# First loads on two queues, another deal of the fill, and attention outputs stored one step later, in a fused two-branch attention layer

## The chip, the cores and the metric

The kernel runs on one core of a Trainium2 chip. A core has a matmul engine (TensorE, PE in the profile; PEld is its weight load), a vector engine (VectorE, DVE), an activation engine (ScalarE, ACT), a general engine (GpSimd, POOL) and SyncE (SP), which here only issues transfers between device memory and on-chip memory (SBUF). Matmuls write to a second on-chip memory, PSUM. The metric is the device time of the whole program in microseconds (us).

## The reference

One layer: normalise the rows of x, project them with one matrix w_in into the q, k, v and gate columns of two attention branches, attend, multiply by the gate, project each branch, merge and project out. There are 1024 prompt tokens and 64 sample tokens, the latter with 512 cached keys. All numbers are float32.

```python
h = rms_norm(x, norm_w) @ w_in
sb_q, sb_k, sb_v, sb_z, cb_q, cb_k, cb_v, cb_z, g_sb, g_cb = split(h)
# branch sb, stick-breaking: z = q.k / 8, keys s < t
w = exp(log_sigmoid(z) + (reverse_cumsum(log_keep) - log_keep))     # log_keep = log_sigmoid(-z) where s < t
o_sb = w @ v
# branch cb: keys of the last 8 chunks of 64 and the own one, softmax with a clipped relative bias
o_cb = softmax(q.k / 8 + rel_bias) @ v                              # q and k with an RMS norm per head
b_sb = (o_sb * silu(z_sb)) @ w_proj_sb
b_cb = (o_cb * silu(z_cb)) @ w_proj_cb
y = x + (sigmoid(g_sb) * b_sb + sigmoid(g_cb) * b_cb) @ w_out
```

## The kernel before

Every float32 matmul operand is split into a high and a low part, and three products of the parts are summed; that is why q, k and the projections exist as pairs of tiles (hi and lo).

The program has three parts. First come the norm and nearly all columns of w_in; the results go to device memory (`d_qT`, `d_kT`, `d_z`, `d_g` and so on). The last four column blocks of w_in, called units, are left over as filler. Then comes the attention, and after it the second branch's projection and the output projection. The change touches the attention part.

**Steps.** The attention runs over a list `seq` of 136 steps, written out by hand: branch sb and then branch cb; in each, four pairs of heads p; in each pair the sample tile (t = 8, both heads in one step) and then the eight prompt tiles t = 0 to 7, once for each head. A pair is 17 steps. Step i issues, in this order: for cb, `soft` of step i-1 and `mid` of step i-2; `qk(i)` (the scores, L1039, into PSUM tiles z, then for sb two sigmoids on ACT and for cb the bias add on DVE); loads for later steps (`load_z` and `prefetch`); for sb, `mid` of step i-1 (the scan on DVE, with its constants in a PSUM tile `imp`, and the product on POOL); `flush`, which issues postponed stores; a piece of fill; the product with v that has come due (`av`, L1134); the transposes of step i-4 (`tr`, L1100, LAG = 4); and another piece of fill. A prompt step of sb has 128(t+1) keys, one of cb at most 640, the sample step 576.

**Fill.** `fill(n)` puts n matmuls of the filler between the attention's own. The filler is the four units (72 matmuls each in three groups of 24, L782) and then `proj_sb`, the first branch's projection (288 matmuls in groups of 12, L881). Seventy-two are issued before step 0. How many follow in each step is the table `plan`. Before the change `plan` comes, for both branches, from a model (`share`) of what a step costs on PE and on the other engines; it deals 168 matmuls to the sb steps and 228 to the cb steps. The last unit's second group may not start before `late["sb"]` is set, since it loads the first branch's outputs (`load_og`, tiles `ot`, L838). Each output is then split by `og_hi` on ACT (L842) and `og_lo` on DVE or POOL (L847), called between filler matmuls (`og_step`). The filler's `ot`, gate (`gt`, L861) and weight (`wraw`, L109) loads are issued as its generator reaches them.

**Queues.** All loads and stores of this part are issued by SP, in program order; an issue that has to wait holds all issues behind it. Of the load helpers, `place_k` and `place_q` issue four transfers each through `rdma` (L51): `ks` (prompt keys, 256 KB each), `kss` (cached and new sample keys, 128 KB and 16 KB each), `sq` (queries of three prompt tiles, 192 KB each) and `sqs` (sample queries, 32 KB each). `load_v` issues three (L735 to L737), `load_z` one gate tile `zt` (L1117). `av` multiplies its result into `zt` (L1139) and postpones the store of that tile (L695). Every transfer takes one of eight completion counters in turn, and it is not issued before the counter's last transfer has landed.

**Start of the attention.** The loads for step 0 and 1 are issued between pieces of 12 filler matmuls, so the filler's own stores and weight load stand between them in SP's order.

## Time and profile before

| | us |
|---|---|
| median of 3 runs | 1021.68 (1019.37 to 1023.84) |
| the profiled execution | 1022.05 |
| its span, first to last instruction | 1020.1 |
| PE idle in the whole span (1020.10 less 970.01 busy) | 50.1 |
| first filler matmul; first score matmul; second score step | 523.26; 535.10; 546.64 |
| second branch's first score step; last score matmul | 692.58; 851.6 |

Outside the span lie 1022.05 - 1020.1 = 1.95 us. A row of the view of waits reads: engine, operation and line that waited, what ended the wait; us in total, times, longest. A row of the view of stretches reads: stretch, its length, busy us (and instructions) of PE, PEld, DVE, ACT and POOL, the clock granted to PE (1.00 is full), busy share of the transfer engines, GB/s. A row of the view in order of time reads: start, length, engine, line, operation, tiles, shapes, count, and in brackets the idle time before it and what ended it. SPq is SP's issue of a transfer; its length is the issue, not the transfer.

### The profile page before, as it was taken

The numbers are of one execution on the slowest core, as the hardware profiler recorded it, in microseconds if no ns is written. First come the engines' busy times: TensorE is split into PE (matmuls) and PEld (weight loads), VectorE is DVE, ScalarE is ACT, GpSimd is POOL, SyncE is SP. The second block draws the span as 40 slices with busy tenths as digits, with TensorE's granted clock in tenths as the row PEclk, the third lists the DMA queues.
The fourth block names the chain that finished last, engine by engine and source line by source line (L and its number), as shares of the span: only waits on it lengthen the run. The fifth ranks groups of instructions, "written<-read, shape, count | busy, mean of one in ns | idle before, by whom it ended". The sixth has DMA issues, their size and how long they took to land.

```text
span 1020.1 us, 20722 instructions
## 1 busy us (share of the span) xinstructions
PE 970.0 (95%) x7616; PEld 919.0 (90%) x7616; DVE 620.3 (61%) x1259; ACT 496.8 (49%) x1110; POOL 426.7 (42%) x432
## 2 busy tenths in 40 slices
PE   5999999999999999999995998999899799999998
PEld 5999999999999999999995777777787787999998
DVE  5466663985545556233214888887677665589735
ACT  6544442444344333333324775776776665456320
POOL 3376663115544445444423655653110100377452
PEclk9999999999999999999997999999999999999999
DMA  6736468335654333334229756767878662663642
GB/s 230 222 124 208 165 239 289 122 103 168 189 164 152 105 114 113 96 97 128 86 82 241 211 155 162 185 168 198 236 201 218 176 180 82 216 209 99 192 130 91
DMA packets 172197, 166.99 MB, mean 164 GB/s; under 512 B 34688, under 2 KB 157952, under 8 KB 171968
## 3 DMA queue, kind: packets, MB, share of 16 engines
q1 hardware_dynamic: 163376, 157.34, 51.8%
q10 hardware_dynamic: 8720, 8.33, 2.5%
q8 instruction: 60, 0.98, 0.4%
q14 instruction: 41, 0.34, 0.1%
HBM read 106.89 MB, written 58.72 MB: 162 GB/s over the span
## 4 chain that ended last, share of the span: by engine, by line
PE 84%; DMA 4%; ACT 4%; SPq 3%; DVE 2%; issue 1%; POOL 0%; ACTq 0%; POOLq 0%; DVEq 0%
PE b L642 29%; PE acc L472 19%; PE b L1485 7%; PE o L1134 7%; PE pt L1100 5%; PE b L923 5%; PE z L1039 4%; PE acc L881 4%; PE acc L782 2%; SPq L51 2%; DMA wraw<-in_w_proj_sb_dram 1%; ACT wT L1109 1%; DVE wT L1111 1%; ACT be L1043 1%; PE pk L357 1%
## 5 line engine op out<-in xcount | busy, mean ns | idle before, releaser
L1069 POOL TENSOR_TENSOR be<-be,kp 128x128 f32<-128x128 f32 (+8 forms) x68 | 82.0, 1206 | 77.3 <-DVE kp L1067 41.3
L1039 PE MATMUL z<-ks,sq 128*128 128x320 f32 (+5 forms) x384 | 88.8, 340 | 13.4 <-DMA d_gcb<-sg 10.3
L1100 PE MATMUL pt<-ident,be 128*128 128x128 f32 (+1 forms) x568 | 89.3, 280 | 8.8 <-DVE wT L1111 4.4
L1100 PEld LDWEIGHTS pt<-ident,be 128*128 128x128 f32 (+1 forms) x568 | 65.1, 141 | 23.1 <-issue 9.7
L122 POOL TENSOR_TENSOR wlo<-wraw,whi 128x1024 fp32r<-128x1024 f32 x18 | 43.6, 2422 | 95.5 <-ACT whi L115 95.3
L1067 DVE TENSOR_TENSOR_SCAN kp<-kp,acc 128x512 f32<-128x512 f32 (+6 forms) x60 | 76.8, 1280 | 2.1
L1039 PEld LDWEIGHTS z<-ks,sq 128*128 128x128 f32 x384 | 63.9, 192 | 15.6 <-DMA sq<-d_qsbT 10.5
L472 PE MATMUL acc<-whi,xa 128*128 128x256 f32 x256 | 74.2, 292 | 0.0
L1134 PE MATMUL o<-wT,vp 128*64 128x256 f32 (+1 forms) x608 | 71.5, 365 | 1.5 <-DVE wT L1111 1.2
L650 DVE TENSOR_TENSOR u<-b,s 128x256 f32<-128x256 f32 (+1 forms) x56 | 24.4, 440 | 78.7 <-PE b L642 77.0
L472 PE MATMUL acc<-wlox,xm 128*128 128x256 f32 x256 | 70.7, 278 | 0.0
L472 PE MATMUL acc<-whi,xm 128*128 128x256 f32 x256 | 70.7, 278 | 0.0
L1111 DVE COPY wT<-pt 128x512 f32<-128x512 f32 (+3 forms) x125 | 63.2, 517 | 12.2 <-PE pt L1100 11.4
L472 PE MATMUL acc<-wlo,xa 128*128 128x256 f32 x256 | 70.7, 278 | 0.0
L472 PE MATMUL acc<-whix,xb 128*128 128x256 f32 x256 | 70.6, 278 | 0.0
L472 PE MATMUL acc<-whix,xm 128*128 128x256 f32 x256 | 70.6, 278 | 0.0
L1134 PEld LDWEIGHTS o<-wT,vp 128*64 128x64 f32 x608 | 45.9, 140 | 25.5 <-issue 6.1
L1042 ACT ACTIVATE kp<-z 128x384 f32<-128x384 f32 (+6 forms) x104 | 52.8, 508 | 23.7 <-PE z L1039 21.2
L1109 ACT ACTIVATE wT<-pt 128x512 f32<-128x512 f32 (+3 forms) x75 | 36.7, 489 | 49.0 <-PE pt L1100 48.8
L442 POOL TENSOR_TENSOR whix<-ws,whix 128x512 fp32r<-128x512 f32 x28 | 37.0, 1320 | 41.9 <-ACT whix L441 41.9
L1043 ACT ACTIVATE be<-z 128x384 f32<-128x384 f32 (+6 forms) x104 | 53.3, 512 | 0.0
L1072 ACT ACTIVATE be<-be,sm 128x640 f32<-128x640 f32 (+5 forms) x68 | 47.1, 693 | 11.4 <-DVE sm L1071 11.3
(299 smaller groups left out, 3225.0 us busy)
## 6 DMA issues: line engine op xcount, KB each, us to landing
wraw<-in_w_in_dram SPq DMA_DIRECT2D x31, 512.0 KB, 4.3
wrawx<-in_w_in_dram SPq DMA_DIRECT2D x17, 512.0 KB, 4.5
sq<-d_qsbT SPq DMA_DIRECT2D x32, 192.0 KB, 3.8
sq<-d_qcbT SPq DMA_DIRECT2D x32, 192.0 KB, 4.8
xt<-in_x_prompt_dram SPq DMA_DIRECT2D x8, 512.0 KB, 5.4
d_kcbT<-hl SPq DMA_DIRECT2D x8, 512.0 KB, 4.6
d_qcbT<-hl SPq DMA_DIRECT2D x8, 512.0 KB, 5.5
d_ksbT<-hl SPq DMA_DIRECT2D x16, 256.0 KB, 2.5
```

What stands on the lines that cost most here:

```text
L472: TE.matmul(ps, x, w, start=m == 0, stop=m == len(steps) - 1)
L642: TE.matmul(ps[:, :m], w[:, hl_, k], right[s](x)[:, k, a:b], start=s < 3 and k == 0 and e == 0, stop=k == 3 and e == 2, skip_group_check=s ...
L923: TE.matmul(pp[uu][:, :n], w[:, p, uu * 128:uu * 128 + 128], g[:, a:e], start=p == 0 and m == 0, stop=p == NPAIR - 1 and m == 2)
L1039: TE.matmul(z[:, :m], s[:, e, q0:q0 + 128], ks[:, h, o + x:o + y], start=e == parts[0][0], stop=e == parts[-1][0])
L1042: A.activation(kp[:r, x:y], z[:r, :m], AF.Sigmoid, scale=-0.125)
L1043: A.activation(be[:r, x:y], z[:r, :m], AF.Sigmoid, scale=0.125)
L1067: V.tensor_tensor_scan(kp[:, m - 1::-1], kp[:, m - 1::-1], imp[:, 192:193].to_broadcast([128, m]), kp[:, m:m + 1], op0=OP.mult, op1=OP.add)
L1069: G.tensor_tensor(out=be[:r, :n], in0=be[:r, :n], in1=kp[:r, 1:n + 1], op=OP.mult)
L1100: TE.transpose(pt[:kr, x, :r], be[:r, kb * 128:kb * 128 + kr], ident[:r, :r])
L1111: V.tensor_copy(w[:, sl:sl + m, q0:q0 + r], pt[:, :m, :r])
L1134: TE.matmul(o[hd * 64:hd * 64 + 64, c0:c1], vv[:kr, kb, hd * 64:hd * 64 + 64], wT[b, p, j, hd, s // 4][:kr, s % 4, c0:c1] if j < 4 else wT ...
L1485: TE.matmul(ps[:, t], left[s](xs_, k)[:, ts_], wt_[:, k], start=s < 3 and t == k == e == 0, stop=k == 3 and e == 2, skip_group_check=s > 2 ...
```

## The change

Four things are changed.

1. The first loads: `rdma`, `place_k`, `place_q`, `load_q` and `load_k` can issue from another engine. All loads for steps 0 and 1 now come before the 72 filler matmuls. `sqs` and `ks` are issued by ACT, the others by SP.
2. The fill: the cb steps get 12 matmuls at once and then 240 more in proportion to the number of keys plus 150 (`need`). The sb steps still go by the model, with 144 instead of 168.
3. The store of an attention output waits for one more `flush` (`store_later(..., 1)`), the tiles `zt` have four buffers instead of three, and `late["sb"]` is set one step later to match.
4. Nothing is added to or taken from the work: 576 filler matmuls in all, 72 ahead and 108 after the steps, as before, up to one by rounding.

The table `plan`, in filler matmuls per pair of 17 steps:

| pair | before | after |
|---|---|---|
| sb 0 / 1 / 2 / 3 | 57 / 37 / 37 / 37 | 51 / 31 / 31 / 31 |
| cb 0 / 1 / 2 / 3 | 55 / 57 / 57 / 59 | 71 / 60 / 60 / 60 |
| cb 1, its 17 steps | 0 0 0 2 0 0 2 8 7 3 8 6 7 0 3 6 5 | 5 1 2 2 2 3 3 4 3 5 4 5 4 4 5 4 4 |

SP at the start of the attention, before. `kss`, `sqs`, `ks` and `sq` are keys and queries of steps 0 and 1, `vp` and `vs` the values, `d_gcb<-sg` the filler's stores, `wraw` the filler's weights; "x4" is four transfers.

```order
L51 DMA kss<-d_csbT_77 64x512 x4
L51 DMA kss<-d_ksbT_69 64x64 x4
L51 DMA sqs<-d_qsbT_61 64x2x64 x4
L695 DMA d_gcb_105<-sg 128x384
L51 DMA ks<-d_ksbT_69 64x1024 x4
L109 DMA wraw<-in_w_in_dram 128x8x128
L51 DMA sq_7093<-d_qsbT_61 64x2x384 x4
L695 DMA d_gcb_105<-sg 128x128
L695 DMA d_gcb_105<-sg 128x32
L695 DMA d_gcb_105<-sg 128x224
L735 DMA vp<-d_sbv 128x8x128
```

SP at the same place, after:

```order
L51 DMA kss<-d_csbT_77 64x512 x4
L51 DMA kss<-d_ksbT_69 64x64 x4
L51 DMA sq_7041<-d_qsbT_61 64x2x384 x4
L735 DMA vp<-d_sbv 128x8x128
L736 DMA vs<-in_cache_sb_v_dram 128x4x128
L737 DMA vs<-d_sbv 64x128
L1117 DMA zt<-d_zsb_85 128x64
L695 DMA d_gcb_105<-sg 128x384
L109 DMA wraw<-in_w_in_dram 128x8x128
L695 DMA d_gcb_105<-sg 128x128
L695 DMA d_gcb_105<-sg 128x32
L695 DMA d_gcb_105<-sg 128x224
```

The other half stands on ACT, after the last evacuation of the part before (`hl`) and ahead of the filler's first evacuation (`sg`). In brackets is what each issue waits for: DMAHW0 to DMAHW7 are the eight completion counters.

```order
L580 ACTIVATE hl<-u_6830 128x288 [waits DMAHW0_49,DMAHW7_49,DVE_49,Activation_49]
L51 DMA sqs<-d_qsbT_61 64x2x64 [waits Pool_49]
L51 DMA sqs<-d_qsbT_61 64x2x64
L51 DMA sqs<-d_qsbT_61 64x2x64 [waits DMAHW1_49]
L51 DMA sqs<-d_qsbT_61 64x2x64 [waits DMAHW3_49]
L51 DMA ks<-d_ksbT_69 64x1024 [waits DMAHW5_49]
L51 DMA ks<-d_ksbT_69 64x1024 [waits DMAHW0_49]
L51 DMA ks<-d_ksbT_69 64x1024 [waits DMAHW3_49]
L51 DMA ks<-d_ksbT_69 64x1024 [waits DMAHW7_49]
L757 ACTIVATE sg<-acc 128x384 [waits PE_49]
```

So `sqs` and `ks` no longer queue behind `kss`, `sq` stands ahead of the filler's traffic, and the values ahead of the filler's weights.

SP between the third and the fourth pair of branch cb, before; `bias` and `bsm` are the bias rows of the next pair, `sqs` the queries that its first step needs:

```order
L51 DMA kss<-d_ccbT_84 64x512 x4
L51 DMA kss<-d_kcbT_84 64x64 x4
L861 DMA gt<-d_gsb_95 128x384
L861 DMA gt<-d_gsb_96 128x384
L109 DMA wraw<-in_w_proj_sb_dram 128x4x256
L1170 DMA bias<-d_rb_123 128x640
L1170 DMA bias<-d_rb_124 128x640
L1178 DMA bsm<-d_rb_123 64x576
L1178 DMA bsm<-d_rb_124 64x576
L695 DMA d_ocb_115<-zt 128x256
L1117 DMA zt<-d_zcb_91 128x256
L51 DMA sqs<-d_qcbT_68 64x2x64 x4
```

and after:

```order
L109 DMA wraw<-in_w_proj_sb_dram 128x4x256
L695 DMA d_ocb_114<-zt 128x256
L1117 DMA zt<-d_zcb_91 128x256
L51 DMA kss<-d_ccbT_84 64x512 x4
L51 DMA kss<-d_kcbT_84 64x64 x4
L695 DMA d_ocb_115<-zt 128x64
L1170 DMA bias<-d_rb_123 128x640
L1170 DMA bias<-d_rb_124 128x640
L1178 DMA bsm<-d_rb_123 64x576
L1178 DMA bsm<-d_rb_124 64x576
L1117 DMA zt<-d_zcb_91 128x256
L51 DMA sqs<-d_qcbT_68 64x2x64 x4
```

The filler's gate and weight loads left the place between `kss` and `sqs`, and the stores `d_ocb` moved behind the loads of the next step.

PE at the first steps of the second pair of cb, before (`z` scores, `o` the product with v, `pt` transposes, `acc` filler):

```order
L1039 MATMUL z<-kss,sqs 128x288 x8
L1134 MATMUL o<-wT,vp 64x256 x8
L1134 MATMUL o<-wT,vp 64x128 x4
L1100 MATMUL pt<-ident,be 128x128 x5
L1039 MATMUL z<-ks,sq_9702 128x128 x2
L1100 MATMUL pt<-ident,be 128x128 x5
L1039 MATMUL z<-ks,sq_9702 128x128 x2
L1100 MATMUL pt<-ident,be 128x128 x5
L1039 MATMUL z<-ks,sq_9702 128x256 x2
L881 MATMUL acc<-xb,whi 128x384
L1100 MATMUL pt<-ident,be 128x128 x5
```

and after:

```order
L1039 MATMUL z<-kss,sqs 128x288 x8
L782 MATMUL acc<-xm,wlo 128x320
L881 MATMUL acc<-xa,whi 128x384
L1134 MATMUL o<-wT,vp 64x256 x8
L1134 MATMUL o<-wT,vp 64x128 x4
L1100 MATMUL pt<-ident,be 128x128 x5
L881 MATMUL acc<-xb,whi 128x384
L881 MATMUL acc<-xa,wlo 128x384
L881 MATMUL acc<-xa,whi 128x384
L1039 MATMUL z<-ks,sq_9685 128x128 x2
L1100 MATMUL pt<-ident,be 128x128 x5
L881 MATMUL acc<-xb,whi 128x384
```

Each short step now has filler of its own.

The diff, with the parts that only pass the engine on left out:

```diff
-    def rdma(out, in_):
+    def rdma(out, in_, eng=SP):
         out, in_ = (a if isinstance(a, bass.AP) else a[:] for a in (out, in_))
-        SP.dma_start(out.bitcast(F32), in_.bitcast(F32))
+        eng.dma_start(out.bitcast(F32), in_.bitcast(F32))
...
-    def store_later(dst, src):
-        deferred.append((0, lambda: SP.dma_start(dst, src)))
+    def store_later(dst, src, n=0):
+        deferred.append((n, lambda: SP.dma_start(dst, src)))
...
-        zt = am.tile([128, 256], F32, name="zt", bufs=3)
+        zt = am.tile([128, 256], F32, name="zt", bufs=4)
...
-        store_later(d_o[b][p][:, 256 * j:256 * j + nq], os[:, :nq])
+        store_later(d_o[b][p][:, 256 * j:256 * j + nq], os[:, :nq], 1)
...
     load_k("sb", 0, 1)
-    for f in (lambda: load_q("sb", 0, 3), lambda: load_k("sb", 0, 0), lambda: load_q("sb", 0, 0),
-              lambda: (load_v("sb", 0), load_z("sb", 0, 4)), lambda: None, lambda: None):
+    load_q("sb", 0, 3, A)
+    load_q("sb", 0, 0)
+    load_k("sb", 0, 0, A)
+    load_v("sb", 0)
+    load_z("sb", 0, 4)
+    for _ in range(6):
         fill(12)
         flush()
-        f()
...
     plan = {}
-    for b, budget in (("sb", 72 * (len(units) - 1) - 48), ("cb", 48 + FP)):
+    steps = [i for i in range(len(seq)) if seq[i][0] == "cb"]
+    need = [band(*seq[i][::2])[1] + 150 for i in steps]
+    acc = 12.0
+    for i, n in zip(steps, need):
+        acc += (60 + FP) * n / sum(need)
+        plan[i] = int(acc)
+        acc -= plan[i]
+    for b, budget in (("sb", 72 * (len(units) - 1) - 72),):
...
-        if i == len(seq) // 2 + LAG + 1:
+        if i == len(seq) // 2 + LAG + 2:
             late["sb"] = True
```

More of the change, by code (lines that the diff above doesn't have):

```diff
@@ L692, in flush, with place_k, place_q @@
                 deferred.append((n - 1, f))
-    def store_later(dst, src):
-        deferred.append((0, lambda: SP.dma_start(dst, src)))
-    def place_k(dst, src, o0, o1, a, b):
+    def store_later(dst, src, n=0):
+        deferred.append((n, lambda: SP.dma_start(dst, src)))
+    def place_k(dst, src, o0, o1, a, b, eng=SP):
         for hd in range(2):
             for m in range(2):
-                rdma(dst[m * 64:m * 64 + 64, hd, a:b], src[hd * 64:hd * 64 + 64, m, o0:o1])
-    def place_q(dst, src, o0, o1):
+                rdma(dst[m * 64:m * 64 + 64, hd, a:b], src[hd * 64:hd * 64 + 64, m, o0:o1], eng)
+    def place_q(dst, src, o0, o1, eng=SP):
         for hd in range(2):
@@ L708, in place_q @@
                 rdma(dst[dup * 64:dup * 64 + 64, 2 * hd:2 * hd + 2, c:c + o1 - o0],
-                     src[hd * 64:hd * 64 + 64, :, o0:o1])
+                     src[hd * 64:hd * 64 + 64, :, o0:o1], eng)
     SQ, KS, VP, BI, st, wT, zts = {}, {}, {}, {}, {}, {}, {}
@@ L738, in load_v, with load_q @@
         VP[b, p] = (vp, vs)
-    def load_q(b, p, ci):
+    def load_q(b, p, ci, eng=SP):
         x, y = CH[ci] if ci < 3 else (NP, T)
@@ L743, in load_q, with load_k @@
             y = min(y, NP)
-        place_q(alloc_q((b, p), ci), d_qT[b][p][:], x, y)
-    def load_k(b, p, s):
+        place_q(alloc_q((b, p), ci), d_qT[b][p][:], x, y, eng)
+    def load_k(b, p, s, eng=SP):
         if s:
@@ L750, in load_k @@
         else:
-            place_k(alloc_k((b, p), 0), d_kT[b][p][:], 0, NP, 0, NP)
+            place_k(alloc_k((b, p), 0), d_kT[b][p][:], 0, NP, 0, NP, eng)
     def ev_act(func, dst, ci, a, b, ps):
```

## The prediction

> **What bounds the kernel now.** I read the page's chain first, then what PE waited for, then the stretches around the long waits, then SP's issues there.

> ```profile
> PE 84%; DMA 4%; ACT 4%; SPq 3%; DVE 2%; issue 1%; POOL 0%; ACTq 0%; POOLq 0%; DVEq 0%
> ```
> ```profile
> PE z L1039 <- DMA d_gcb<-sg: 10.3, 1, 10.3
> ...
> PE z L1039 <- DMA sqs<-d_qcbT: 4.9, 1, 4.9
> PE pt L1100 <- DVE wT L1111: 4.4, 9, 0.8
> ...
> PE z L1039 <- DVE sm L1045: 1.8, 1, 1.8
> ...
> PE z L1039 <- DMA sq<-d_qcbT: 1.3, 2, 1.1
> ```

> PE carries 84% of the chain, so the change can only win by filling PE's holes; it removes no matmul. The rows shown lie in the attention, at places that the change touches. How large the holes are, with the slow clock behind them, the stretches show:

> ```profile
> 535.10:546.64 11.54, 1.21 (x10) 1.00 (x9) 2.37 (x6) 1.75 (x5) 1.24 (x2) 0.71 1.02 225
> 546.64:550.20 3.56, 3.56 (x13) 3.56 (x14) 0.84 (x2) 0.89 (x4) 0.45 (x2) 0.51 0.99 278
> ...
> 722.80:727.20 4.40, 1.67 (x8) 0.69 (x6) 2.31 (x9) 4.17 (x9) 0.29 (x2) 1.00 1.02 302
> 727.20:732.00 4.80, 4.78 (x24) 3.24 (x24) 2.22 (x8) 3.18 (x7) 2.29 (x4) 0.64 0.55 157
> ...
> 810.30:815.20 4.90, 0.00 (x0) 0.01 (x1) 0.84 (x3) 1.32 (x3) 1.92 (x5) 0.77 0.48 122
> 815.20:818.50 3.30, 3.28 (x14) 2.64 (x16) 0.99 (x4) 0.00 (x0) 1.01 (x1) 0.50 0.89 247
> 818.50:822.00 3.50, 3.31 (x29) 2.20 (x25) 0.75 (x4) 0.43 (x1) 0.00 (x0) 0.82 0.95 255
> ```

> **Term 1, the first loads.** SP's issues in order of time:

> ```profile
> 525.36 2.43 SPq L51 DMA_DIRECT2D kss<-d_csbT  x4
> 527.83 2.52 SPq L51 DMA_DIRECT2D kss<-d_ksbT  x4
> 530.45 3.15 SPq L51 DMA_DIRECT2D sqs<-d_qsbT  x4
> 533.70 0.53 SPq L695 DMA_DIRECT2D d_gcb<-sg  x1
> 534.28 2.38 SPq L51 DMA_DIRECT2D ks<-d_ksbT  x4
> 536.71 0.59 SPq L109 DMA_DIRECT2D wraw<-in_w_in_dram  x1
> 537.34 2.75 SPq L51 DMA_DIRECT2D sq<-d_qsbT  x4
> 540.19 2.60 SPq L695 DMA_DIRECT2D d_gcb<-sg  x3
> 545.22 0.37 SPq L735 DMA_DIRECT2D vp<-d_sbv  x1
> ```
> ```profile
> 525.00:530.00 5.00, 5.00 (x30) 5.00 (x30) 0.00 (x0) 1.44 (x2) 0.80 (x1) 1.00 0.44 140
> 530.00:535.00 5.00, 5.00 (x35) 5.00 (x34) 0.00 (x0) 0.49 (x1) 1.66 (x3) 1.00 0.22 56
> 535.00:540.00 5.00, 1.31 (x10) 1.08 (x8) 2.37 (x6) 1.75 (x5) 1.14 (x2) 0.99 0.94 230
> ...
> 555.00:560.00 5.00, 4.88 (x34) 3.89 (x32) 4.50 (x9) 4.58 (x12) 3.39 (x7) 1.00 1.05 241
> ```

> An issue takes about 0.6 us (2.43/4). The large transfers (`ks`, 1 MB; `sq`, 0.77 MB) stand behind `kss`, `sqs` and filler traffic, so the transfer engines idle until 534 (0.44 and 0.22 busy) and are then full, still so in 555 to 560. PE pays in 535 to 547. The values `vp` were issued at 545.22, which is when `wraw`, eight places ahead, had landed.

> ```profile
> 527.68 0.49 ACT L757 ACTIVATE sg<-acc 128x384 f32<-128x384 f32 x1 [3.23 <-PE acc L782]
> ```

> After, ACT is free at 524.45 (this first evacuation of the filler stood behind 3.23 us of idle time). It issues four `sqs` (to about 527) and four `ks`, of which the last waits for the fourth `kss`; ACT is done by about 531. The evacuation then comes some 3 us late; the third filler group needs its bank only 48 matmuls after the first one's start at 523.26 (row under term 5), about 531.5, so this is just covered, and if the cover fails the third group starts 1 to 2 us late, inside the wait that is left. SP issues `sq` from about 531.5. So 2.5 MB (0.58 `kss`, 0.13 `sqs`, `ks`, `sq`) must move from 526 on; at 230 to 241 GB/s that takes 11 us, to 537, and PE, which arrives at 536.3, would gain up to 9.6 us at the second step (546.64 to 537).

> But the transfers stay full. The step at t = 3 needs the next `sq` (0.77 MB), which SP issues behind values (0.83 MB), filler stores (0.54) and `wraw` (0.52), before as after:

> ```profile
> 554.86 0.63 PE L1039 MATMUL z<-ks,sq 128*128 128x512 f32 x2
> ```

> All bytes ahead of that step are the same; what is won is the idle transfer time: (240 - 140) x 3.5 us and (240 - 56) x 5 us are 0.35 + 0.92 MB, at 240 GB/s 5.3 us. I take -6, nearer to this row than to the other end, since a part of 546 to 555 was PE at 0.51 of its clock (1.7 us lost), which need not come back. Ends: 0 (the wait only moves) and -10.

> **Term 2, the hole at 810.** The chain there (view in order of time) and what SP waited for in 795 to 830:

> ```profile
> 804.13 7.64 DMA wraw<-in_w_proj_sb_dram
> 811.79 3.29 DMA sqs<-d_qcbT
> 815.22 2.26 PE z L1039 x8
> ```
> ```profile
> SPq L1117 <- DMA d_ocb<-zt: 3.6, 1, 3.6
> SPq L51 <- DMA wraw<-in_w_proj_sb_dram: 2.4, 1, 2.4
> ```

> `sqs` waits for its counter, held by the 512 KB `wraw`, and SP was late by a `zt` load that waited for the store out of its buffer. After, `wraw` stands ahead of `kss` and not between `kss` and `sqs` (2.4 us), and a `zt` buffer comes round a turn later, so its store has long landed (3.6 us). Together 6.0 us against a hole of 4.95: gone. With it goes the slow clock: 3.3 x 0.50 + 3.5 x 0.18 = 2.3 us. That is at most -7.2; I take -6.5. At least 0, if `kss` now waits where `sqs` did.

> **Term 3, the hole at 723.**

> ```profile
> 723.03 0.52 ACT L842 ACTIVATE xa<-ot 128x384 fp32r<-128x384 f32 x1 [3.56 <-DMA ot<-d_osb]
> ```

> ACT stood 3.56 us for a reloaded output, behind it the softmax of that step, then DVE, then PE: 4.40 - 1.67 = 2.7 us idle and 4.8 x 0.36 = 1.7 us of clock, 4.4 in all. Load and use lie 18 filler matmuls apart; these were dealt at 6 to 8 a step and are now dealt at about 4.4, so the load has four steps instead of two or three. I take -3 (0 to -4.4). The rows show 0.64 of the clock behind 2.7 us of holes, the longest 1.8. [...]

> **Term 4, the later stores.**

> ```profile
> SPq L695 <- DVE zt L1139: 27.2, 7, 7.0
> SPq L1117 <- DMA d_ocb<-zt: 16.5, 7, 3.8
> ```

> SP stood 27 us for attention outputs not yet computed, with loads behind them. A step later the output is there. Stores themselves are read only by `ot` loads, and the gate `late["sb"]` moves along: some 3 filler matmuls wait one step, below 0.5 us, hidden by the attention's own. On PE only the 1.3 us at `sq` show this: -1.3 (0 to -1.3).

> **Term 5, the moved fill.** A filler matmul takes 0.164 us (72 from 523.26 to 535.10):

> ```profile
> 523.26 0.33 PE L782 MATMUL acc<-xa,whi 128*128 128x384 f32 x1
> ...
> 535.10 1.22 PE L1039 MATMUL z<-kss,sqs 128*128 128x288 f32 x8
> ```
> ```profile
> 600.00:610.00 10.00, 10.00 (x69) 8.53 (x68) 9.86 (x12) 8.64 (x22) 5.89 (x8) 1.00 0.54 149
> ...
> 760.00:770.00 10.00, 10.00 (x76) 9.02 (x75) 8.49 (x29) 7.51 (x16) 0.29 (x2) 1.00 0.66 205
> ```

> Twenty-four matmuls, 3.9 us, leave sb. There DVE is as full as PE in the long steps (9.86), so about half comes back: -2. They enter cb, where PE is full (10.00 beside 8.49): +3.9. Inside cb some 12 per pair move from the steps with t = 3 and more to the short ones at a pair's head. Of PE's 4.4 us of small holes before transposes (the row of waits above) a good half lies there, and I take -2 for filling it, and the long steps come nearer to DVE's pace (+1.5). Sum +1.5. Ends: -2, and +11.6 where sb returns nothing and the 44 matmuls fewer in the long steps of cb (7.2 us) and some holes (0.5) shorten nothing (3.9 + 7.2 + 0.5).

> **Sum.** -6 - 6.5 - 3 - 1.3 + 1.5 = -15.3 against the profiled execution's 1022.05: 1006.8. The median of the runs lies 0.4 lower, so 1006.4; I say 1007.

> **Rivals.**
> *Two queues don't help* (term 1 is 0). For it: the transfers are full from 535 to 560, and the counters still let only eight be under way on both queues together. Against it: 0.44 and 0.22 busy before. Time: 1022.05 - 9.3 = 1012.8. [...]
> *The hole at 810 moves* (terms 2 and 4 are 0): `kss` waits for `wraw` and PE for `kss`. For it: the 2.4 us that SP waited there were a wait for transfers under way, not for a result. Time: 1022.05 - 6 - 3 + 1.5 = 1014.6.
> *ACT is held by `ot` loads more often: slower.* ACT is in order, and each hold like that at 723 costs PE 4.4 us. Twelve outputs are split in this way. With n holds instead of one the time is 1022.05 - 12.3 + 4.4 (n - 1); from n = 5 on it is slower by over 0.5%; at six, 1031.8. For it: the last output's store is later, and `ot` follows `kss` in SP's order. Against: only one of twelve held ACT long, and the uses are now further apart.

> **Chances.** Forecast 0.52 (its own range 1002 to 1011), two queues don't help 0.14, the hole moves 0.19, ACT held 0.08, the fill's bad end (1022.05 - 16.8 + 11.6 = 1016.9) 0.07. Faster by over 0.5% (5.1 us, about what a measurement of this kernel can tell from no change) is below 1016.6: the forecast, the first rival, three quarters of the second, which lies 2 us inside: 0.80; I put 0.79. Slower 0.09, the rest within. Range: 1000 (terms 1 to 4 at -10, -7.2, -4.4, -1.3 and 5 at +1.5 give 1000.7) to 1018 (above the bad end of the fill).

> **What would show it.** Right: the second score step starts at 537 to 541, and a PE wait for `sq` of 1 to 3 us follows at t = 3; no PE wait for `sqs` over 1 us in cb; SP's wait for `zt` on DVE below 10 us; cb's stretches at PE 9.5 and more, also at the pair heads. Wrong: the clock at 0.5 after the first step again, ACT waiting for `ot` more than once, or DVE near 10 and PE at 9 in cb's long steps.

## The result, and the profile after

| | before | after |
|---|---|---|
| median of the runs, us | 1021.8 (1019.37 to 1023.84) | 1004.12 (1002.67 to 1004.53) |
| profiled execution; its span | 1022.05; 1020.1 | 1003.83; 1002.0 |
| mean clock granted to PE | 0.988 | 0.996 |

The ratio is 0.9825 with a 95% interval of 0.9801 to 0.9849: 17.7 us faster, 2.9 us below the forecast of 1007 and inside its range. The prediction was right on the time, and in the size of two of its five terms, the first loads and the hole at 810.

Where the time went is read from marks that both traces have: the first filler matmul (L782), the first score step of each pair, the first matmul of the second branch's projection (L923) and the end.

| stretch | before | after | difference |
|---|---|---|---|
| ahead of the first filler matmul (the change touches nothing there) | 523.26 | 524.77 | +1.5 |
| to the second pair of sb | 54.13 | 48.31 | -5.8 |
| to the first pair of cb (sb 1, 2, 3; 18 filler matmuls fewer) | 115.19 | 114.39 | -0.8 |
| first pair of cb (16 more) | 44.56 | 43.08 | -1.5 |
| second pair (3 more) | 35.65 | 35.04 | -0.6 |
| third pair | 42.43 | 35.43 | -7.0 |
| from the fourth pair to L923 | 70.16 | 66.04 | -4.1 |
| from L923 to the end | 134.72 | 134.94 | +0.2 |
| span | 1020.1 | 1002.0 | -18.1 |

The 1.5 us ahead of the filler are scatter: this mark lies between 523.9 and 525.1 in the eight experiments too, and before's is the earliest of all. Each stretch is read from one execution: the start, 54.13 us before, takes 53.00 and 55.04 us in two kernels below whose first loads are the same. So a difference of 1 or 2 us in one row need not be the change's work. That holds for 1.7 of the 4.1 us from the fourth pair on. PE waits just ahead of L923 for `xm`, which DVE writes from a filler result (L885), 2.18 us before and 2.42 after; before, the clock was at 0.50 for the 3.41 us behind that wait (881.23 to 884.64), and after it was 1.00 there (865.13 to 868.54). The last section shows why that is luck.

PE's share of the chain rose from 84% to 87%; what PE waited for from 500 to 870 us (total, times, longest, in us) is now:

```profile
PE 87%; DVE 4%; DMA 3%; ACT 3%; issue 2%; SPq 1%; POOL 0%; ACTq 0%; DVEq 0%; POOLq 0%
```
```profile
PE acc L782 <- ACT sg L757: 4.3, 5, 2.5
...
PE acc L881 <- DVE xm L885: 2.4, 1, 2.4
...
PE z L1039 <- DMA sq<-d_qsbT: 2.1, 1, 2.1
...
PE z L1039 <- DVE sm L1045: 1.3, 1, 1.3
...
PE z L1039 <- DMA sq<-d_qcbT: 0.5, 2, 0.3
```

The two largest waits of before, 10.3 us for the first loads and 4.9 us for `sqs`, are gone. The first loads in order of time, on SP, then on ACT, then what PE did meanwhile:

```profile
526.98 2.71 SPq L51 DMA_DIRECT2D kss<-d_csbT  x4
529.73 3.36 SPq L51 DMA_DIRECT2D kss<-d_ksbT  x4
533.19 3.30 SPq L51 DMA_DIRECT2D sq<-d_qsbT  x4
...
545.79 5.20 SPq L51 DMA_DIRECT2D sq<-d_qsbT  x8
```
```profile
525.54 2.56 ACTq L51 DMA_DIRECT2D sqs<-d_qsbT  x4
528.13 7.07 ACTq L51 DMA_DIRECT2D ks<-d_ksbT  x4
535.25 0.49 ACT L757 ACTIVATE sg<-acc 128x384 f32<-128x384 f32 x1 [9.29 <-DMA ks<-d_ksbT]
```
```profile
535.79 0.42 PE L782 MATMUL acc<-xa,whi 128*128 128x320 f32 x1 [2.48 <-ACT sg L757]
...
539.43 1.22 PE L1039 MATMUL z<-kss,sqs 128*128 128x288 f32 x8
540.49 0.34 PE L1039 MATMUL z<-ks,sq 128*128 128x128 f32 x2
...
550.40 0.70 PE L1039 MATMUL z<-ks,sq 128*128 128x512 f32 x2 [2.07 <-DMA sq<-d_qsbT]
```

The second score step starts at 540.49 (before: 546.64). Two shorter waits took the place of the long one: 2.48 us ahead of the third filler group, since ACT stood in its own issues until 535.2, and 2.07 us for the next `sq`, whose issues began only at 545.79. In stretches (length, busy us of PE, PEld, DVE, ACT, POOL, clock, transfer share, GB/s):

```profile
530.00:535.00 5.00, 3.32 (x19) 2.99 (x18) 0.00 (x0) 0.00 (x0) 0.00 (x0) 1.00 1.00 222
535.00:540.00 5.00, 4.21 (x29) 4.21 (x30) 0.00 (x0) 2.19 (x4) 2.47 (x3) 1.00 0.96 227
...
545.00:550.00 5.00, 2.95 (x32) 2.14 (x30) 4.05 (x9) 2.38 (x7) 2.71 (x9) 1.00 0.73 204
550.00:555.00 5.00, 4.60 (x18) 4.15 (x18) 1.77 (x3) 2.45 (x5) 1.79 (x4) 0.66 1.01 249
...
720.00:725.00 5.00, 2.83 (x22) 2.19 (x19) 2.68 (x11) 3.59 (x7) 1.32 (x5) 1.00 0.97 301
725.00:730.55 5.55, 5.55 (x33) 5.51 (x31) 4.73 (x19) 5.32 (x12) 2.25 (x3) 0.69 0.68 188
```

The transfers are full from 530 to 555 but for 0.73 in 545 to 550 (before, 530 to 535 had 0.22). The last two rows are a hole that did not go: the one at 723, now at 721, with the slow clock behind it as before. ACT's row there, and SP's around the load that ACT waited for:

```profile
720.81 0.53 ACT L842 ACTIVATE xa<-ot 128x384 fp32r<-128x384 f32 x1 [3.11 <-DMA ot<-d_osb]
```
```profile
709.61 2.37 SPq L51 DMA_DIRECT2D kss<-d_ccbT  x4
712.02 4.69 SPq L51 DMA_DIRECT2D kss<-d_kcbT  x4
716.81 1.37 SPq L695 DMA_DIRECT2D d_ocb<-zt  x1
718.28 0.38 SPq L838 DMA_DIRECT2D ot<-d_osb  x1
```

### The profile page after: what moved, and what is told of

Its sections match the earlier page's. It is cut to its first block, busy times and chain, and to the rows that moved or that the text cites. A ratio compares the mean times of both kernels' runs of the same rounds, so it can differ in the third digit from the quotient of the medians.

```text
span 1002.0 us, 20702 instructions
## 1 busy us (share of the span) xinstructions
PE 967.0 (97%) x7616; PEld 916.1 (91%) x7616; DVE 623.1 (62%) x1259; ACT 495.2 (49%) x1110; POOL 426.3 (43%) x432
## 4 chain that ended last, share of the span: by engine, by line
PE 87%; DVE 4%; DMA 3%; ACT 3%; issue 2%; SPq 1%; POOL 0%; ACTq 0%; DVEq 0%; POOLq 0%
PE b L642 29%; PE acc L472 19%; PE b L1495 8%; PE o L1134 6%; PE pt L1100 5%; PE z L1039 5%; PE b L923 5%; PE acc L881 4%; PE acc L782 3%; DVE kp L1067 1%; DVE wT L1111 1%; PE pk L357 1%; DMA wrawx<-in_w_in_dram 1%; PE pt L285 1%; PE acc L1531 1%
## 5 line engine op out<-in xcount | busy, mean ns | idle before, releaser
L1100 PE MATMUL pt<-ident,be 128*128 128x128 f32 (+1 forms) x568 | 89.6, 281 | 8.1 <-DVE wT L1111 2.9
L1039 PE MATMUL z<-ks,sq 128*128 128x320 f32 (+5 forms) x384 | 87.4, 337 | 3.9 <-DMA sq<-d_qsbT 2.1
L1100 PEld LDWEIGHTS pt<-ident,be 128*128 128x128 f32 (+1 forms) x568 | 65.4, 141 | 22.4 <-issue 10.0
L1111 DVE COPY wT<-pt 128x512 f32<-128x512 f32 (+3 forms) x125 | 63.3, 517 | 12.9 <-PE pt L1100 12.0
L1039 PEld LDWEIGHTS z<-ks,sq 128*128 128x128 f32 x384 | 64.7, 191 | 6.3 <-issue 3.3
L1134 PE MATMUL o<-wT,vp 128*64 128x256 f32 (+1 forms) x608 | 68.5, 357 | 1.2 <-DVE wT L1111 0.8
L1134 PEld LDWEIGHTS o<-wT,vp 128*64 128x64 f32 x608 | 43.8, 136 | 25.0 <-issue 5.0
```

Of the source, the lines that this page charges most:

```text
L1039: TE.matmul(z[:, :m], s[:, e, q0:q0 + 128], ks[:, h, o + x:o + y], start=e == parts[0][0], stop=e == parts[-1][0])
L1100: TE.transpose(pt[:kr, x, :r], be[:r, kb * 128:kb * 128 + kr], ident[:r, :r])
L1111: V.tensor_copy(w[:, sl:sl + m, q0:q0 + r], pt[:, :m, :r])
L1134: TE.matmul(o[hd * 64:hd * 64 + 64, c0:c1], vv[:kr, kb, hd * 64:hd * 64 + 64], wT[b, p, j, hd, s // 4][:kr, s % 4, c0:c1] if j < 4 else wT ...
```

## The experiments

Eight kernels were run. Medians of the kernel before beside them were 1022.36 us (the first loads, the deal, the later stores, the next queries) and 1021.63 us (the other four). "Start" below is the stretch from the first filler matmul to the second pair of sb: 54.13 us before, 48.31 after.

**The first loads alone.** The kernel before with this only:

```diff
...
-    for f in (lambda: load_q("sb", 0, 3), lambda: load_k("sb", 0, 0), lambda: load_q("sb", 0, 0),
-              lambda: (load_v("sb", 0), load_z("sb", 0, 4)), lambda: None, lambda: None):
+    load_q("sb", 0, 3, A)
+    load_q("sb", 0, 0)
+    load_k("sb", 0, 0, A)
+    load_v("sb", 0)
+    load_z("sb", 0, 4)
+    for _ in range(6):
         fill(12)
         flush()
-        f()
```

> The kernel before with the first loads of the change alone (ahead of the filler, sqs and ks issued by ACT). Theory (term 1): the stretch from the first filler matmul (523.26 before) to the second pair's first score step is shorter by about 6 us, as between the kernels before and after (54.1 to 48.3), and everything later stays: the hole before the fourth pair of cb is still near 5 us. Time 1016, that is 6 below before. Rival (what came back there is due to fewer filler matmuls, six of which left the first pair): 1 us of those 6 is the fill's, time 1017; rival (two queues don't help, the gain came from the order of the later loads): within 2 us of before.

Measured: 1015.75 us, ratio 0.9939 (0.9919 to 0.9958), 6.6 us faster. The start took 47.98 us, 6.15 less than before. What PE waited for between 800 and 812:

```profile
PE z L1039 <- DMA sqs<-d_qcbT: 3.0, 1, 3.0
```

The hole ahead of the fourth pair of cb is still there, though at 3.0 us and not near the 5 expected (before: 4.9). So the first term stands by itself, and the rival in which these loads win nothing falls. How much of it is the order and how much the second queue, a later run asks.

**The new deal of the fill alone.** Only `plan` is as after:

```diff
-    for b, budget in (("sb", 72 * (len(units) - 1) - 48), ("cb", 48 + FP)):
+    steps = [i for i in range(len(seq)) if seq[i][0] == "cb"]
+    need = [band(*seq[i][::2])[1] + 150 for i in steps]
+    acc = 12.0
...
+    for b, budget in (("sb", 72 * (len(units) - 1) - 72),):
```

> The kernel before with the new deal of the filler alone. Theory (terms 2, 3, 5): wraw no longer stands between kss and sqs, so the hole of 4.95 us before the fourth pair shrinks by about 2.4 us to 2 to 3 us but the clock still falls behind it; the moved filler itself costs 1 to 2 us; time 1019 to 1022. Rival (the deal is what won in cb, by filling the short steps): the hole is gone and cb's four pairs are shorter by 10 us or more, time 1008 to 1012.

Measured: 1016.54 us, ratio 0.9944 (0.9924 to 0.9965), 5.8 us faster: between the two times expected. The first, third and fourth pair of cb are 3.5, 4.7 and 3.6 us shorter, the second 6.1 longer. The wait for `sqs` ahead of the fourth pair shrank to 0.6 us, but a new one opened a pair earlier. PE's wait between 765 and 778, and SP there:

```profile
PE z L1039 <- DMA sqs<-d_qcbT: 4.6, 1, 4.6
```
```profile
769.58 1.00 SPq L861 DMA_DIRECT2D gt<-d_gsb  x2
770.68 0.38 SPq L695 DMA_DIRECT2D d_ocb<-zt  x1
771.10 0.43 SPq L1117 DMA_DIRECT2D zt<-d_zcb  x1
771.57 2.47 SPq L51 DMA_DIRECT2D sqs<-d_qcbT  x4
```

PE wanted `sqs` at 770.5 and SP issued it at 771.57, with no `wraw` in its way: it had been held at a `zt` load whose buffer was still being stored (4.2 us, the longest such wait from 750 to 778). The deal moves the hole; it does not close it. So the 5.8 us are a balance of holes that closed and one that opened.

**The later stores alone.** The kernel before with the store a step later, four `zt` buffers and the later gate:

```diff
-        zt = am.tile([128, 256], F32, name="zt", bufs=3)
+        zt = am.tile([128, 256], F32, name="zt", bufs=4)
...
-        store_later(d_o[b][p][:, 256 * j:256 * j + nq], os[:, :nq])
+        store_later(d_o[b][p][:, 256 * j:256 * j + nq], os[:, :nq], 1)
...
-        if i == len(seq) // 2 + LAG + 1:
+        if i == len(seq) // 2 + LAG + 2:
```

> The kernel before with the later stores, the fourth zt buffer and the later gate alone. Theory (terms 2 and 4): SP no longer waits for the store out of the zt buffer (16.5 us of waits on line L1117 go below 3), kss and sqs are issued 3.6 us sooner, so the hole of 4.95 us before the fourth pair shrinks to 1 to 1.5 us and the clock behind it stays; the 1.3 us at sq go: time 1014 to 1017. Rival (wraw between kss and sqs sets the hole, not the buffer): the hole stays above 4 us, time 1020 to 1022.

Measured: 1011.71 us, ratio 0.9888 (0.9866 to 0.9909), 10.6 us faster, the largest of the three parts. PE waits for `sqs` nowhere. From the third pair of cb to L923 it takes 102.45 us (before 112.59), and the first pair of cb 41.51 (before 44.56). The hole at 723 is smaller but there, and the clock stays full behind it:

```profile
720.00:725.00 5.00, 3.29 (x20) 2.30 (x18) 2.07 (x7) 3.93 (x9) 0.29 (x2) 1.00 0.95 282
725.00:730.00 5.00, 4.71 (x36) 3.86 (x37) 3.90 (x17) 4.09 (x9) 2.31 (x4) 1.00 0.74 202
```

The three parts alone give 6.6, 5.8 and 10.6 us, 23.0 together, and all of them in one 17.7: the deal and the stores win part of the same time.

**The fourth `zt` buffer alone.** Of the edits just shown, only the first:

> The kernel before with a fourth zt buffer and nothing else. Theory (the zt loads' waits on the store out of their buffer, 16.5 us on SP in cb, make SP late, and the hole before the fourth pair with it): those waits go below 3 us, the hole of 4.95 us shrinks to below 1.5, time 1012 to 1015, most of what the later stores gave. Rival (the delay by a step counts, since SP still waits 27 us for outputs not yet computed): the hole stays above 3 us, time 1019 to 1022.

Measured: 1014.16 us, ratio 0.9926 (0.9908 to 0.9943), 7.5 us faster. SP's waits for stores out of `zt` buffers (16.5 us in cb before) are gone. From the third pair of cb to L923: 103.36 us, 9.2 less than before, and PE has no wait for `sqs` or `sq` there. SP ahead of the fourth pair, before and then with the buffer:

```profile
804.13 0.38 SPq L109 DMA_DIRECT2D wraw<-in_w_proj_sb_dram  x1
...
808.81 5.05 SPq L51 DMA_DIRECT2D sqs<-d_qcbT  x4
```
```profile
797.29 0.38 SPq L109 DMA_DIRECT2D wraw<-in_w_proj_sb_dram  x1
...
801.30 4.40 SPq L51 DMA_DIRECT2D sqs<-d_qcbT  x4
```

`wraw` still stands ahead of `sqs`, and the four `sqs` still take 4.4 us to issue. But the pair before starts at 772.79 and 775.97, so SP reaches this `wraw` 31.3 us behind it without the buffer and 21.3 with it. The same transfers in the same order do no harm when SP is 10 us earlier. The hole at 723 is untouched (first pair of cb 45.20), and the clock falls behind it:

```profile
725.00:730.00 5.00, 2.61 (x12) 1.22 (x12) 2.45 (x9) 4.31 (x9) 0.58 (x4) 0.80 1.01 299
730.00:735.00 5.00, 5.00 (x23) 3.52 (x24) 2.06 (x7) 3.03 (x7) 2.00 (x2) 0.52 0.60 180
```

SP's wait for outputs not yet computed even rose:

```profile
SPq L695 <- DVE zt L1139: 38.9, 9, 7.0
```

From 500 to 870 it is 27.2 us before, 28.9 after and 38.9 here, without cost on PE. What stores and gate add to the buffer lies, in these two traces, mostly in the first pair of cb: 41.51 against 45.20 us. But the traced execution with the later stores took 3.15 us less than its median (1008.56 against 1011.71), and this one 1.65 us more (1015.81 against 1014.16). By the medians the later stores win 2.45 us more than the buffer, and the two intervals touch.

**The old deal in the kernel after.** Loads and stores as after, `plan` as before:

> The changed kernel with the old deal of the filler: loads and stores alone. Theory (the stores already close the holes in cb, the deal adds little): the two parts alone gave 6.6 and 10.6 us, so 1004 to 1006, within 2 us of the changed kernel. Rival (the deal is worth the 5.8 us that it gave alone): 1008 to 1011.

Measured: 1005.83 us, ratio 0.9858 (0.9834 to 0.9881); after has 0.9825, and the intervals overlap. Stretch by stretch against after, in the order of the table from "start" on: 47.89, 115.19, 41.36, 36.10, 35.83, 68.09 us. So the new deal costs 0.4 and 1.7 us at the start and in the first pair of cb, and wins 0.8, 1.1, 0.4 and 2.05 elsewhere: 2.2 in these stretches, 1.4 by the spans, 1.7 by the medians. By the times the deal can't be told from nothing. The two largest of these differences, 1.7 in the first pair and 2.05 from the fourth on, are each mostly one slot of 3.41 us at half clock (1.7 us), which the one execution had there and the other had not (last section): after had it from 725.18 to 728.59, behind its hole in the first pair, where with the old deal the clock was 1.00 from 705 to 728.4; the old deal had it from 864.16 to 867.57, behind the wait ahead of L923, where after had 1.00. Of the 2.6 us that the 16 matmuls more in the first pair take, 1.6 went where PE had been idle before; the first 7.5 us of that pair before, and then in the kernel after:

```profile
692.58:700.00 7.42, 6.30 (x51) 5.49 (x50) 6.56 (x13) 2.92 (x5) 3.99 (x2) 1.00 0.89 233
```
```profile
687.47:695.00 7.53, 7.53 (x60) 6.39 (x59) 6.12 (x10) 2.06 (x5) 4.13 (x4) 1.00 0.89 222
```

**All first loads on SP.** The kernel after without the second queue, in the same order:

```diff
-    load_q("sb", 0, 3, A)
+    load_q("sb", 0, 3)
     load_q("sb", 0, 0)
-    load_k("sb", 0, 0, A)
+    load_k("sb", 0, 0)
```

> The changed kernel with all first loads on SP in the same order (kss, sqs, sq, ks, values), none on ACT. Theory (the order counts, the second queue saves issue time that stands ahead of 1.8 MB): eight issues of 0.6 us return to SP ahead of sq and ks, so the second score step comes 2 to 4 us later than in the changed kernel (540.5 less 524.8 is 15.7 us after the first filler matmul), at 18 to 20, while the third filler group no longer waits 2.48 us for ACT; at the second pair the difference is 1 to 3 us: time 1005 to 1007. Rival (the second queue is what gained): the 5.8 us of that stretch are lost, 1010. Rival (the second queue only costs, by holding ACT): 1002 or below.

Measured: 1007.38 us (1003.26 to 1011.3), ratio 0.9861 (0.9834 to 0.9887). The start took 50.45 us. SP, then PE's second score step, then the transfers (the number before the last):

```profile
531.72 3.01 SPq L51 DMA_DIRECT2D sqs<-d_qsbT  x4
...
537.35 2.52 SPq L51 DMA_DIRECT2D ks<-d_ksbT  x4
```
```profile
543.08 0.69 PE L1039 MATMUL z<-ks,sq 128*128 128x128 f32 x2 [5.43 <-DMA ks<-d_ksbT]
```
```profile
530.00:535.00 5.00, 5.00 (x33) 5.00 (x32) 0.00 (x0) 0.91 (x2) 2.46 (x3) 1.00 0.20 52
```

So the order of the loads, all of them ahead of the filler's traffic, wins 3.7 of the 5.8 us in these traces, and the second queue 2.1. The times don't confirm the second part: the two kernels are 3.3 us apart by the medians but their intervals overlap, and a start with the same first loads varied by 2 us (53.00 to 55.04). What the rows do show is what the second queue did here. With it the transfers start about 5 us earlier (0.20 busy here against 1.00 from 530 to 535): the first `ks` issue began at 537.35 here and at 528.13 on ACT. PE then waits 2.48 us for ACT.

**The next queries first.** The kernel after, with the `sq` for t = 3 to 5 issued ahead of the filler too:

```diff
     load_z("sb", 0, 4)
+    load_q("sb", 0, 1)
     for _ in range(6):
...
         if t == 8:
-            load_q(b, p, 1)
+            if (b, p) != ("sb", 0):
+                load_q(b, p, 1)
```

> The changed kernel with the queries of the tiles t = 3 to 5 of the first pair loaded ahead of the filler's stores and weights (issued before the 72 filler matmuls). Theory (the bytes ahead of the step t = 3 set when it starts): 1.06 MB fewer stand ahead of it, so the wait of 2.07 us at t = 3 goes and with it the lower clock after it (0.83 in 550 to 560, 1.7 us): time 1000 to 1001. Rival (the transfers are full, so the wait only moves to the next load, the filler's weights or the next pair's keys): a PE wait of 1 us or more appears elsewhere before 570, time 1003 to 1004.5.

Measured: 1002.74 us, ratio 0.9809 (0.9788 to 0.9831). The wait of 2.07 us at t = 3 and the slow clock behind it are gone, and the start is 45.75 us, 2.6 less than after. Of this 1.4 us stay by the medians, and the intervals overlap. In this trace nothing stays of it (its span is 1002.1 us, after's 1002.0): a wait of 1.0 us for `sqs` came back in cb, and the clock fell for one slot behind the wait of 2.52 us ahead of L923: PE's matmuls of one shape (128x320) follow each other there every 0.27 us from 862.86 to 866.06, and every 0.15 us before and after that.

```profile
PE z L1039 <- DMA sqs<-d_qcbT: 1.0, 1, 1.0
```

**Both sets of outputs loaded together.** The previous kernel, with the two sets of `ot` loads issued together, ahead of the eight `kss` issues:

```diff
-                    ots[ci, p] = stage.tile([128, 384], F32, name="ot", bufs=4)
+                    ots[ci, p] = stage.tile([128, 384], F32, name="ot", bufs=8)
...
                             load_og("sb", 0, late["y"])
+                            load_og("sb", 1, late["y"])
...
-            if f is og_hi and p and ci < 2:
+            if f is og_hi and p and ci == 1:
...
```

> The changed kernel with the queries for t = 3 first (as in the run before) and with eight ot buffers, so that the second set of outputs is loaded together with the first and not behind the eight kss issues. Theory (ACT's hold of 3.11 us at 721 is SP's eight kss issues, 7 us, ahead of the load): ACT does not wait for ot in the second set, the PE holes of 1.29 and 0.88 us at 722 and the clock of 0.83 in 720 to 730 go, 3 to 4 us: time 999 to 1000. Rival (the four loads more delay kss and sqs, and a wait for these takes the place): 1002 to 1004.

Measured: 1000.64 us (999.06 to 1001.35), ratio 0.9791 (0.9772 to 0.981): faster than before. It is also 3.5 us below after and 2.1 below the previous kernel by the medians, though the intervals overlap with both. The first pair of cb has no hole: 39.0 us against 41.88 in the previous kernel and 43.08 in after. But the third set of outputs now holds ACT in the second pair, which takes 38.7 us instead of 36.79 and 35.04:

```profile
730.48 0.47 ACT L843 ACTIVATE xa<-ot 128x320 fp32r<-128x320 f32 x1 [3.41 <-DMA ot<-d_osb]
```

## Why the prediction was right, and where it was not

**Term 1, the first loads: right.** It said -6; the start shows -5.8 in the change and -6.15 with the loads alone. The step at t = 3 waited 2.07 us (forecast 1 to 3), and the second score step came at 540.49 (537 to 541). Its working had one bad step: "ACT is done by about 531". ACT was done at 535.20. The counters are one set of eight for both queues: the 872 transfers of this trace, 827 issued by SP and 45 by ACT, landed 109 on each of eight, with at most eight under way. The last `ks` issue went out only at 534.75, when the counter that it needed was given back by a `kss` load of SP, which landed at 534.73. "This is just covered" is therefore wrong: the third filler group was 2.48 us late. As the prediction said of that case, the delay lies inside the wait that was left: the second score step came in the forecast time and has no wait of its own.

**Term 2, the hole at 810: right that it goes, wrong in what closes it.** The sum was 2.4 us for `wraw` moved away and 3.6 us for the buffer. The buffer alone closes the hole, with `wraw` where it was; moving `wraw` and the gate loads alone closed it but for 0.6 us and opened another of 4.6 a pair earlier. These were not two parts to be added: how far SP lagged behind PE decided here, and the buffer cut that lag by 10 us (31.3 to 21.3).

**Term 3, the hole at 723: wrong.** It was to shrink by 3 us, because load and use lay 18 filler matmuls apart and these were dealt more thinly. ACT was held 3.11 us instead of 3.56. The load stands behind eight `kss` issues (709.61 to 716.71) and a store, so it goes out when SP gets there, at 718.28; ACT was free at 717.7. With the old, denser deal in the kernel after the load stands at the same place and ACT is held 2.52 us, no longer than with the new one. With the loads moved ahead of the `kss` issues, in the last experiment, PE's hole is gone. Hole and clock cost 1.3 + 0.9 + 5.55 x 0.31 = 3.9 us after, 4.4 before.

**Term 4, the later stores: wrong in its reading.** The 1.3 us at `sq` did go, but the fourth buffer alone takes them: 4.95 for the hole, 1.3 for `sq` and 2.3 of clock are 8.55 of its 9.2 us in that stretch. SP's wait on DVE was to fall below 10 us and rose. What the stores win beyond the buffer (10.6 against 7.5 us) the prediction had not seen: in the two traces 3.7 us lie in the first pair of cb, where with the buffer alone the clock fell to 0.80 and 0.52 behind the hole, and with the later stores it did not fall. Two slots at half clock (5 x 0.20 + 5 x 0.48 us) are 3.4 of these 3.7 us. With the buffer alone a hole of 1.90 us (725.77 to 727.67) lay in one slot; with the later stores PE's holes were 0.97 and 0.96 us, and the clock was 1.00 throughout. Where the slots lay in that execution its rows don't show, so how much of this is the smaller hole is open, and so is what the stores win in other executions beyond the medians.

**Term 5, the moved fill: not borne out, inside its ends.** It said +1.5; between the kernel after with the old deal and with the new one it is -1.7 by the medians, not told from zero, so even its sign is open. Sb returned 0.8 of the 2 us named. The 16 matmuls that entered the first pair of cb (2.6 us) were priced as if PE were full there. But PE had been idle 1.12 us in 692.58 to 700 and 0.45 in 700 to 710, and is idle for none of it now. The pair is 1.7 us longer than with the old deal, about what the slot at half clock behind the hole at 721 costs; with the old deal the hole was smaller and the clock stayed (PE idle 1.37 us in 715 to 720, clock 1.00; after 2.17 us in 721 to 725, then 0.66 in 725 to 730). From the fourth pair on 2.05 us came back, of which 1.7 are such a slot in the trace with the old deal.

**The sum.** Over the stretches that the change touches it was -19.6 (-18.1 less the +1.5 ahead of them), against -15.3. Third and fourth pair gave -11.1 where terms 2 and 4 had -7.8. This is most of the excess. Of the 3.3 us, 1.7 are the slot at half clock ahead of the end of that stretch, which before had and after had not. So the total is better than its parts, and that is luck: term 3 gave 0.5 instead of 3 us, and the fill, which was to cost 1.5, and the place of that slot made it up. Of the rivals, "two queues don't help" fell in the first run. "The hole moves" held only for the deal alone, "ACT held more often" nowhere: one long hold, as before. The fill's bad end did not come.

## What to carry to other kernels

When a load comes late, look first at how far its issuing queue lags behind the engine that it feeds, and at the oldest wait that made it lag: one more buffer on another tile was worth 7.5 us here, and the transfers just ahead of the late load did no harm once the queue lagged 10 us less. Spacing work further apart did not bring a load forward here, since other loads stood ahead of it in program order: ACT was held 3.11 us with the new deal and 2.52 with the old. The second issuing queue won 2.1 us of the start in these traces, where issues and not bytes had held the transfers back (0.20 busy from 530 to 535 without it); but its engine stood still while it issued and waited to issue, 7.07 us for four loads. And before a difference of 1 or 2 us between two traces is explained, look whether the clock fell in one and not in the other, which was worth 1.7 us a time here.

## What was not expected of the hardware

```profile
534.03:537.45 3.42, 1.66 (x11) 1.66 (x12) 0.00 (x0) 1.82 (x3) 0.68 (x1) 1.00 0.89 212
537.45:540.86 3.41, 3.41 (x26) 3.41 (x25) 0.69 (x3) 1.09 (x4) 1.79 (x3) 1.00 1.08 233
...
547.69:551.10 3.41, 1.34 (x8) 0.94 (x6) 1.86 (x4) 0.80 (x2) 1.81 (x4) 1.00 0.94 244
551.10:554.51 3.41, 3.41 (x14) 3.02 (x13) 1.43 (x2) 2.22 (x5) 1.04 (x2) 0.50 1.02 261
...
861.71:865.13 3.42, 1.69 (x11) 1.69 (x12) 2.10 (x3) 0.01 (x1) 0.79 (x1) 1.00 0.09 16
865.13:868.54 3.41, 3.41 (x24) 3.41 (x23) 0.98 (x2) 1.70 (x2) 0.00 (x0) 1.00 0.85 276
```

The same place as the last two, ahead of L923, in the kernel after with the old deal:

```profile
860.75:864.16 3.41, 1.10 (x8) 0.92 (x7) 2.57 (x4) 0.97 (x2) 1.28 (x2) 1.00 0.10 35
864.16:867.57 3.41, 3.41 (x15) 3.41 (x14) 0.49 (x1) 1.06 (x1) 0.00 (x0) 0.50 0.75 234
```

The wait of 2.48 us (533.31 to 535.79) is parted by the mark at 534.03; 1.76 us of it lie in one slot, and the clock stays. The wait of 2.07 us (548.33 to 550.40) lies in one slot, and the clock falls. The wait ahead of L923 is 2.42 us after, parted so that 1.73 lie in one slot, and the clock stays. With the old deal it is shorter, 2.31 us, but all of it lies in one slot, and the clock falls. Before, 2.18 us lay in one slot (877.81 to 881.23), and it fell. Counted over the traces of before and after from 30 us on, 562 whole slots at full clock have a whole slot behind them. The six that were followed by one at 0.50 had 1.81 to 3.41 us of PE's idle time, the other 556 at most 1.76. Six falls are too few to read a limit from. A slot at 0.50 in which PE is busy loses 3.41 x 0.50 = 1.7 us. Of the two waits of 2.07 and 2.48 us in the kernel after, the shorter one therefore cost these 1.7 us on top and the longer one nothing, according to where the marks fell. They fell differently in the two traces: counted back from the falls in steps of 3.41 us, the first comes 0.59 us after the first instruction before and 1.55 us after it in the kernel after.
